# Gate projection of each head interleaved with the attention items

## The chip, the cores and the metric

The kernel runs on one core of a Trainium2 chip. The metric is the device time of one execution in microseconds (us); less is better. Engines: TensorE (PE) does matmuls into eight accumulator banks, VectorE (DVE), ScalarE (ACT) and GpSimd (POOL) work on elements, and the queues of SyncE (SP) and POOL issue the transfers.

## What is computed

One inference step with two layers, on 512 latent and 128 context tokens of width 2048. Layer 0 is attention with 16 query heads, 4 key and value heads and a gate; layer 1 is a gated recurrence, which the change does not touch. Cut from the reference:

```python
p = h @ w_in
q, k, v, g = split(p, [2048, 2560, 3072])      # widths 2048, 512, 512, 2048
q = rms_norm(q per head); k = rms_norm(k per head)
q = rope(q); k = rope(k)                       # latent tokens only
o = softmax(q k^T * HD**-0.5) v                # context: 128 keys; latent: 256 cached + 512 latent
out = (o * silu(g)) @ w_out
```

A latent token reads the 256 cached keys and its own 512; a context token reads the 128 context keys. Each sub-layer is led by a norm with shift and scale, which come from `silu(c) @ w_mod + b_mod`.

## The kernel before

Everything is float32. A product is made of three matmuls: every operand is split into a high part, rounded to TensorE's fast format, and a low part (operand less high part), and high x high, low x high and high x low are added in the accumulator (`mm3`, lines 184 to 186). `split_w` makes the two parts of a weight block: a cast on ACT (L179) and a subtraction on DVE (L180). The normed input of layer 0 stands as `hi` and `lo`, [128, 16, 644], in which every head of the attention result later takes the place of one sixteenth (latent tokens in columns 0 to 511, context tokens in 514 to 641).

The stretch that matters runs in stages. **Projections**: `gemm_nat` makes v, k and four blocks of 512 query columns in tokens x columns, in pairs of token tiles; `norm_rope` (from L454) copies each pair, squares it, reduces it per head (L463), scales it (L466), rotates it (L471 to L478) and stores it to DRAM (`q_s`, `k_s`; L485 on POOL's queue). The last pair is the single context tile. Its working tiles have two buffers. **Gate columns**: `gemm_T` makes eight blocks of 256 gate columns as columns x tokens, two accumulators of 322 tokens each per head; `g_evac` (L487) makes `g * (1 + tanh(g / 2))` and stores it per head to `g_s` in DRAM. **Attention**: 72 items, four query tiles of each of 16 heads and after each second head one item for the context tokens of both. Three functions treat an item: `stage_s` (L597) writes the scores into one of two 2-bank tiles `sp` and issues the softmax (maximum on DVE, L581; exponential on ACT, L584; normalisation on ACT or DVE by item); `stage_t` (L619) transposes the probabilities on TensorE and splits them; `stage_v` (L646), which works for two query tiles together, and so only at m = 1, 3 and 4 of a head's five kinds of item, multiplies with v and, at m = 3 and 4, with the gate (L664, L670), writing `hi` (L665, ACT) and `lo` (L666, POOL). The transposes of an item stand three items behind its scores (`AHEAD`). **Output projection** with `w_out` starts when the items are done and reads all of `hi` and `lo`.

Beside the projections and the gate columns runs `gemv` (L379), the vector product of the conditioning with `w_mod` for layer 1's shift and scale, as products on DVE: four blocks of 1024 columns, eight loads of 1 MB each, 16 partial sums per column and vector accumulated in place (L395). A block's 128 partition sums are then reduced on TensorE: the sums are split, eight matmuls of 512 columns with a selector (L403), a row copy on ACT (L406), eight transposes (L408). `background` spreads the loads over the projections and the gate columns.

Instructions of an engine run in the order in which they stand; a scheduler sets that order from the program and a priority. Loads of weights, of w_mod and of attention's inputs share four tiles `raw` of 1 MB.

## Time and profile before

| | us |
|---|---|
| median of 3 runs (lowest, highest) | 1954.33 (1953.74, 1959.88) |
| the profiled execution's own time | 1955.32 |
| its span | 1953.6 |
| PE busy | 1883.5 (96%) |
| DVE busy | 1323.9 (68%) |
| ACT busy | 865.0 (44%) |
| POOL busy | 133.1 (7%) |
| mean granted clock of TensorE, share of full | 0.991 |

In the trace the projections of layer 0 end at 428.69 us, the gate columns run to 664.6, the attention from there to 884.08, when the output projection begins. Times in the rows are microseconds from the start of the span; a row of a timeline has the start, the duration, the engine, the line, the operation, the tile written and the tiles read, the shapes and a count, and in brackets the idle time before it with what ended it. Matmuls overlap, so the time of one in a row of them is the distance between starts.

### The profile page before, as it was taken

How to read it: one execution, taken by the hardware profiler on the slowest of the kernel's cores; microseconds unless marked ns; L12 is line 12 of the kernel's file. 1: busy time of each engine (PE TensorE's matmuls, PEld its weight loads, DVE VectorE, ACT ScalarE, POOL GpSimd, SP SyncE). 2: the span in 40 equal slices, each digit the busy share in tenths (PEclk: the TensorE clock that was granted, in tenths of full speed). 3: DMA queues.
4: the chain of work that ended last, by engine and by line, in shares of the span. 5: the costliest groups of instructions: out<-in, count | busy, mean ns of one | idle time of the engine just before them, and what ended most of it. 6: DMA issues, size and time to landing. Idle time of an engine off the chain costs nothing.

```text
span 1953.6 us, 26764 instructions
## 1 busy us (share of the span) xinstructions
PE 1883.5 (96%) x10857; PEld 1673.2 (86%) x10857; DVE 1323.9 (68%) x1846; ACT 865.0 (44%) x1255; POOL 133.1 (7%) x212
## 2 busy tenths in 40 slices
PE   4999999999999899999999989899999999999996
PEld 1567887879999899998888889899999999987885
DVE  3237759758375389998857774875685675798645
ACT  4441223222121388881223565666456456742232
POOL 0000000000000001110000000110010010020000
PEclk9999999999999999999999999999999999999998
DMA  9996535536454212225636673323232232546445
GB/s 342 343 318 209 166 109 183 178 123 200 149 178 158 74 38 74 74 97 174 204 130 211 226 263 109 122 77 117 94 102 92 94 100 64 175 140 212 146 149 216
DMA packets 194892, 304.20 MB, mean 156 GB/s; under 512 B 7232, under 2 KB 124608, under 8 KB 191952
## 3 DMA queue, kind: packets, MB, share of 16 engines
q1 hardware_dynamic: 188800, 276.20, 42.6%
q0 software_dynamic: 5968, 26.28, 3.7%
q8 instruction: 85, 1.39, 0.3%
q14 instruction: 39, 0.32, 0.0%
HBM read 273.03 MB, written 29.43 MB: 155 GB/s over the span
## 4 chain that ended last, share of the span: by engine, by line
PE 83%; DVE 6%; ACT 5%; issue 2%; DMA 2%; SPq 1%; POOL 0%; DVEq 0%; ACTq 0%; POOLq 0%
PE pd L184 22%; PE pd L185 22%; PE pd L186 22%; PE pd L215 2%; PE pm L276 2%; PE pd L217 2%; PE pd L218 2%; PE ph L631 1%; PE pg L184 1%; ACT L937 1%; PE pg L186 1%; PE pg L185 1%; PE sp L184 1%; PE sp L186 1%; PE ph L184 1%
## 5 line engine op out<-in xcount | busy, mean ns | idle before, releaser
L179 ACT CAST wh<-raw 128x1024 fp32r<-128x1024 f32 x248 | 258.1, 1048 | 604.8 <-PE pd L186 323.6
L180 DVE TENSOR_TENSOR wl<-raw,wh 128x1024 fp32r<-128x1024 f32 x248 | 301.4, 1221 | 237.5 <-ACT wh L179 236.6
L184 PE MATMUL pd<-wh,hi 128*128 128x512 f32 x1040 | 410.4, 395 | 5.8 <-ACT pd L783 3.3
L185 PE MATMUL pd<-wl,hi 128*128 128x512 f32 x1040 | 409.9, 394 | 0.0
L186 PE MATMUL pd<-wh,lo 128*128 128x512 f32 x1040 | 409.7, 394 | 0.0
L184 PE MATMUL pd<-hi,wh 128*128 128x322 f32 x1280 | 399.2, 312 | 0.0
L186 PE MATMUL pd<-hi,wl 128*128 128x322 f32 x1280 | 397.0, 310 | 1.1 <-DVE wl L180 1.1
L185 PE MATMUL pd<-lo,wh 128*128 128x322 f32 x1280 | 397.5, 311 | 0.0
L186 PEld LDWEIGHTS pd<-hi,wl 128*128 128x128 f32 x1280 | 241.6, 189 | 1.6 <-DVE wl L180 1.6
L185 PEld LDWEIGHTS pd<-lo,wh 128*128 128x128 f32 x1280 | 242.2, 189 | 0.1
L184 PEld LDWEIGHTS pd<-hi,wh 128*128 128x128 f32 x1280 | 241.4, 189 | 0.5 <-ACT wh L179 0.3
L184 PEld LDWEIGHTS pd<-wh,hi 128*128 128x128 f32 x1040 | 195.5, 188 | 52.5 <-ACT pd L783 3.7
L186 PEld LDWEIGHTS pd<-wh,lo 128*128 128x128 f32 x1040 | 195.4, 188 | 45.9
L185 PEld LDWEIGHTS pd<-wl,hi 128*128 128x128 f32 x1040 | 195.4, 188 | 45.4 <-DVE wl L180 0.3
L741 DVE SCALAR_TENSOR_TENSOR ga<-raw,cT,ga 128x512 f32<-128x512 f32 x256 | 175.5, 744 | 15.2 <-DMA ga<-b_mod 12.4
L395 DVE SCALAR_TENSOR_TENSOR ga<-raw,cT,ga 128x1024 f32<-128x1024 f32 x120 | 149.7, 1278 | 28.1 <-DMA raw<-w_mod 27.5
L215 PE MATMUL pd<-hi,wh 128*128 128x256 f32 (+1 forms) x256 | 80.5, 314 | 6.4 <-ACT wh L179 4.7
L184 PE MATMUL pd<-xh,wh 128*128 128x322 f32 x256 | 81.1, 318 | 5.2 <-ACT xh L875 4.4
L185 PE MATMUL pd<-xl,wh 128*128 128x322 f32 x256 | 80.0, 313 | 0.0
L218 PE MATMUL pd<-hi,wl 128*128 128x256 f32 (+1 forms) x256 | 79.9, 312 | 0.0
L217 PE MATMUL pd<-lo,wh 128*128 128x256 f32 (+1 forms) x256 | 79.8, 312 | 0.0
L186 PE MATMUL pd<-xh,wl 128*128 128x322 f32 x256 | 79.8, 312 | 0.0
(233 smaller groups left out, 2807.3 us busy)
## 6 DMA issues: line engine op xcount, KB each, us to landing
raw<-w_mod SPq DMA_DIRECT2D x64, 1024.0 KB, 5.2
raw<-w_in_lru SPq DMA_DIRECT2D x40, 1024.0 KB, 5.3
raw<-w_in_attn SPq DMA_DIRECT2D x36, 1024.0 KB, 6.1
raw<-w_mod SPq DMA_DIRECT2D x64, 512.0 KB, 8.4
raw<-w_out_attn SPq DMA_DIRECT2D x20, 1024.0 KB, 6.0
raw<-w_out_lru SPq DMA_DIRECT2D x20, 1024.0 KB, 5.3
g_s<-qf POOLq DMA_DIRECT2D x16, 322.0 KB, 3.4
raw<-g_s SPq DMA_DIRECT2D x16, 322.0 KB
```

Of the source, the lines that this page charges most:

```text
L179: S.copy(wh, src)
L180: V.tensor_tensor(wl, src, wh.bitcast(F32), op=sub)
L184: PE.matmul(out, ah, bh, start=first, stop=False)
L185: PE.matmul(out, ah, bl, start=False, stop=False)
L186: PE.matmul(out, al, bh, start=False, stop=last)
L215: PE.matmul(outs[f], wh[:, c], hi[:, k, t], start=(k == 0 and first[f]), stop=False, skip_group_check=True)
L217: PE.matmul(outs[f], wh[:, c], lo[:, k, t], start=False, stop=False, skip_group_check=True)
L218: PE.matmul(outs[f], wl[:, c], hi[:, k, t], start=False, stop=(k == KT - 1), skip_group_check=True)
L276: PE.matmul(pm[32 * j:32 * j + 32], c32[:, kb * 4 + j], raw[:, j * 512:j * 512 + 512], start=(kb == 0), stop=(kb == 3))
L395: V.scalar_tensor_tensor(acc[c], w2[:, k2], cT[:, k, c:c + 1], acc[c], op0=mult, op1=add)
L631: PE.transpose(pt[:, c * 128:c * 128 + 128], P[:, b, c * 128:c * 128 + 128], ident)
L741: V.scalar_tensor_tensor(acc[:, c], raw[:, k4 * 512:k4 * 512 + 512], cT[:, kb * 4 + k4, c:c + 1], acc[:, c], op0=mult, op1=add)
```

## The change

The gate columns no longer have a stage of their own. A generator, `gate`, issues the 96 matmuls of one head after the other (16 weight blocks x 3, for each half of 322 tokens), with one accumulator bank per half; a head's weights are one load of 16 x 128 columns. The program calls `fill(n)`, which issues the next n gate matmuls, between the parts of the attention: 44 ahead of the first scores, and in each step 9 after the scores, 8 after the values and 8 after the transposes. The order of TensorE's instructions is that of the code; the other engines' order is still the scheduler's. The tile of scores has one buffer, probabilities two, their split transposes one, keys one. The gate of a head stays on chip (five buffers `gg`). Because gate matmuls still read `hi` and `lo`, the finished heads go to DRAM (`a_s`) until the gate has ended; then `load_a` fetches one head per step, with a cast on ACT into `hi` and a subtraction on POOL into `lo`. Heads whose values come after that are written straight away (`direct`). Transposes now stand one step, values two steps behind the scores.

`gemv` is called twice: shift beside the projections, in blocks of 1024, and scale beside the attention, in blocks of 512. Its reduction is now fp32 matmuls with two columns of the selector as the moving side.

```diff
@@ -31,10 +31,9 @@
 EPS = 1e-6
 QSCALE = HD ** -0.5
 NORM = "dadad"
-AHEAD = 3
-QV = (1, 2, 3)
-QO = (2, 2, 3)
-PB = 4
+GGB = 5
+LEAD = 44
+FILL = (9, 8, 8)
 GATE2 = (1, 2, 5)
...
-    g_s = [tc.dram_tile([128, TW], F32, name=f"g_s{h}") for h in range(NH)]
+    a_s = [tc.dram_tile([128, TW], F32, name=f"a_s{h}") for h in range(NH)]
...
+    def gemv(part, p, ps_, width):
+
+        nk, nf = 2048 // width, width // 128
+        for col in range(0, D, width):
+            acc = [p.tile([128, width], F32, name=f"ga{c}", tag=f"ga{c}") for c in range(2)]
+            for kb in range(KT // nk):
+                w = rawp.tile([128, 2048], F32, name="raw", tag="raw")
+                wk = w.rearrange("p (k n) -> p k n", k=nk)
+                SY.dma_start(wk, i["w_mod"][1, kb * nk * 128:(kb + 1) * nk * 128,
+                                            part * D + col:part * D + col + width]
+                             .rearrange("(k p) n -> p k n", p=128))
+                for k2 in range(nk):
+                    k = kb * nk + k2
+                    for c in range(2):
+                        if k == 0:
+                            V.tensor_scalar(acc[c], wk[:, k2], cT[:, k, c:c + 1], None, op0=mult)
+                        else:
+                            V.scalar_tensor_tensor(acc[c], wk[:, k2], cT[:, k, c:c + 1], acc[c],
+                                                   op0=mult, op1=add)
+                    if k2 % 2 or nk == 2:
+                        yield
...
+            pg = ps_()
+            for k in range(nf):
                 for c in range(2):
...
+                    PE.matmul(pg[:, 2 * k:2 * k + 2], acc[c][:, k * 128:k * 128 + 128],
+                              sel[:, c].bitcast(F32), start=(c == 0), stop=(c == 1))
...
+    gv = gemv(0, pb, lambda: psd()[:, 0], 1024)
...
-        credit[0] += 32 / 36
+        credit[0] += 32 / 19
...
-    def g_evac(acc, gb):
-        for f in range(2):
-            th = pb.tile([128, 2, 512], F32, name="qs", tag="qs", bufs=2)
-            gg = pb.tile([128, 2, 512], F32, name="qf", tag="qf", bufs=2)
-            S.activation(th[:, :, :TH], acc[f][:, :, :TH], AF.Tanh, scale=0.5)
-            V.scalar_tensor_tensor(gg[:, :, :TH], th[:, :, :TH], 1.0, acc[f][:, :, :TH], op0=add, op1=mult)
-            G.dma_start(g_s[gb * 2 + f].rearrange("p (h t) -> p h t", h=2), gg[:, :, :TH])
...
-    for gb in range(8):
-        g_evac(gemm_T(w_in, 3072 + gb * 256, background), gb)
...
-    psS = pool("psS", 2, PSUM, stack=xs)
+    psS = pool("psS", 1, PSUM, stack=xs)
...
+    psG = pool("psG2", 2, PSUM, stack=xs)
...
+    ggs, over, direct = {}, [], {}
+
+    def gate():
+
+        raws, ws = {}, {}
+
+        def load(h):
+            raws[h] = rawp.tile([128, 2048], F32, name="raw", tag="raw")
+            SY.dma_start(raws[h].rearrange("p (k n) -> p k n", k=KT),
+                         w_in[:, 3072 + h * 128:3200 + h * 128].rearrange("(k p) n -> p k n", p=128))
+
+        def split(h, half):
+            ws[h, half] = split_w(raws[h][:, half * 1024:half * 1024 + 1024])
+
+        load(0)
+        split(0, 0)
+        for h in range(NH):
+            if h + 1 < NH:
+                load(h + 1)
+            gg = pc_.tile([128, TW], F32, name="gg", tag="gg", bufs=GGB)
+            for e in range(2):
+                t = slice(e * TH, e * TH + TH)
+                acc = psG.tile([128, 512], F32, name="pg", tag="pg")
+                for q, half in enumerate((e, 1 - e)):
+                    if (e, q) == (0, 0):
+                        split(h, 1)
+                    elif (e, q) == (1, 0) and h + 1 < NH:
+                        split(h + 1, 0)
+                    wh, wl = ws[h, half]
+                    for k8 in range(8):
+                        k = half * 8 + k8
+                        c = slice(k8 * 128, k8 * 128 + 128)
+                        for n, (x, y) in enumerate(((wh, hi), (wh, lo), (wl, hi))):
+                            PE.matmul(acc[:, :TH], x[:, c], y[:, k, t], start=(q == 0 and k8 == 0 and n == 0),
+                                      stop=(q == 1 and k8 == 7 and n == 2))
+                            yield
+                S.activation(gg[:, t], acc[:, :TH], AF.Tanh, scale=0.5)
+                V.scalar_tensor_tensor(gg[:, t], gg[:, t], 1.0, acc[:, :TH], op0=add, op1=mult)
+            ggs[h] = gg
+        over.append(1)
+
+    gf = gate()
+
+    def fill(n):
+        for _ in range(n):
+            next(gf, None)
...
+    def load_kv(j):
         c = slice(j * 128, j * 128 + 128)
         raw = rawp.tile([128, 2048], F32, name="raw", tag="raw")
-        kx = raw[:, :896].rearrange("p (t d) -> p t d", d=128)
-        vx = pc_.tile([128, 7, 128], F32, name="vx", tag="vx")
-        for x, cache, scr in ((kx, "cache_k", k_s), (vx, "cache_v", v_s)):
-            SY.dma_start(x[:, 0:2], i[cache][0, 0, :, j, :].rearrange("(t p) d -> p t d", p=128))
-            SY.dma_start(x[:, 2:7], scr[:, c].rearrange("(t p) d -> p t d", p=128))
-        kh = pc_.tile([128, 896], F32R, name="kh", tag="kh", bufs=2)
-        kl = pc_.tile([128, 896], F32R, name="kl", tag="kl", bufs=2)
+        x2 = raw[:, :1792].rearrange("p (a t d) -> p a t d", a=2, d=128)
+        for a, (cache, scr) in enumerate((("cache_k", k_s), ("cache_v", v_s))):
+            SY.dma_start(x2[:, a, 0:2], i[cache][0, 0, :, j, :].rearrange("(t p) d -> p t d", p=128))
+            SY.dma_start(x2[:, a, 2:7], scr[:, c].rearrange("(t p) d -> p t d", p=128))
+        kraw[j] = x2
...
+    def load_q(h):
+        qx = pc_.tile([128, 5, 128], F32, name="qx", tag="qx")
+        SY.dma_start(qx, q_s[:, h * 128:h * 128 + 128].rearrange("(t p) d -> p t d", p=128))
+        qraw[h] = qx
...
+        while h not in ggs:
+            fill(1)
+        if m == 1:
+            direct[h] = bool(over)
+        vh, vl = vs[h // 4]
+        po = psh()
+
+        def put_y(h, t, p):
+            y = ggs[h][:, t]
+            V.scalar_tensor_tensor(y, p, 0.5, y, op0=mult, op1=mult)
+            if direct[h]:
+                S.copy(hi[:, h, t], y)
+                G.tensor_tensor(lo[:, h, t], y, hi[:, h, t].bitcast(F32), op=sub)
...
+            for e in range(2):
+                put_y(h - 1 + e, slice(PO, TE), po[:, e * 128:e * 128 + 128])
+                if not direct[h - 1 + e]:
+                    G.dma_start(a_s[h - 1 + e][:, :TE], ggs[h - 1 + e][:, :TE])
+
+    back = iter(range(NH))
+
+    def load_a():
+
+        h = next(back, None)
+        if h is None or direct.get(h):
             return
-        yv = qs_[h][3]
-        if m == 3:
-            V.scalar_tensor_tensor(yv, po, 0.5, qs_[h][2][:, :512], op0=mult, op1=mult)
-            S.copy(hi[:, h, :512], yv)
-            G.tensor_tensor(lo[:, h, :512], yv, hi[:, h, :512].bitcast(F32), op=sub)
-        else:
-            h0 = h - 1
-            for e in range(2):
-                V.scalar_tensor_tensor(yv[:, e * 128:e * 128 + 128], po[:, e * 128:e * 128 + 128], 0.5,
-                                       qs_[h0 + e][2][:, PO:TE], op0=mult, op1=mult)
-            y2 = yv[:, :256].rearrange("p (h t) -> p h t", h=2)
-            S.copy(hi[:, h0:h0 + 2, PO:TE], y2)
-            V.tensor_tensor(lo[:, h0:h0 + 2, PO:TE], y2, hi[:, h0:h0 + 2, PO:TE].bitcast(F32), op=sub)
+        raw = rawp.tile([128, 2048], F32, name="raw", tag="raw")
+        r = raw[:, :TE]
+        SY.dma_start(r, a_s[h][:, :TE])
+        S.copy(hi[:, h, :TE], r)
+        G.tensor_tensor(lo[:, h, :TE], r, hi[:, h, :TE].bitcast(F32), op=sub)
...
+    gv = gemv(1, pc_, psh, 512)
+    with tc.manual_schedule(engines={mybir.EngineType.PE}):
+        load_kv(0)
+        load_q(0)
+        fill(LEAD - 12)
+        attn_k(0)
+        attn_q(0)
+        fill(12)
+        for n in range(len(items) + 2):
+            it = items[n] if n < len(items) else None
+            if it:
+                h, m = it
+                if m == 0 and h + 1 < NH:
+                    load_q(h + 1)
+                    if h % 4 == 3:
+                        load_kv(h // 4 + 1)
+                stage_s(it)
+                if it == last[h] and h + 1 < NH:
+                    if h % 4 == 3:
+                        attn_k(h // 4 + 1)
+                    attn_q(h + 1)
+            fill(FILL[0])
+            if n >= 2:
+                h, m = items[n - 2]
+                if m == 0 and h % 4 == 0:
+                    attn_v(h // 4)
+                stage_v((h, m), *done.pop(n - 2))
+            fill(FILL[1])
+            if 0 <= n - 1 < len(items):
+                done[n - 1] = stage_t(items[n - 1])
+            fill(FILL[2])
+            if n % 2:
+                next(gv, None)
+            if over:
+                load_a()
+        for _ in gv:
+            pass
+        for _ in range(NH):
+            load_a()
```

DVE at the start of the attention, the last query block's norm (its last step is L475) up to the low parts of the first head's keys (`kl`) and queries (`ql`); `ga` are sums of the vector product. In the changed kernel the first maximum (L614) stands three vector products behind these rows:

```order
L461 TENSOR_TENSOR qf<-qf,rr 128x512
L475 TENSOR_TENSOR qs<-qf,gain_q 128x512
L393 TENSOR_SCALAR ga_3303<-raw,cT 128x512
L393 TENSOR_SCALAR ga_3304<-raw,cT 128x512
L579 TENSOR_TENSOR kl<-ph,kh 128x512
L579 TENSOR_TENSOR kl<-ph,kh 128x384
L395 SCALAR_TENSOR_TENSOR ga_3303<-raw,cT,ga_3303 128x512
L395 SCALAR_TENSOR_TENSOR ga_3304<-raw,cT,ga_3304 128x512
L395 SCALAR_TENSOR_TENSOR ga_3303<-raw,cT,ga_3303 128x512
L607 TENSOR_TENSOR ql<-ph,qh 128x512
L607 TENSOR_TENSOR ql<-ph,qh 128x128
```

Before, the first maximum (L581) follows at the end of the gate columns; `wl<-ph` is the low part of the queries:

```order
L492 SCALAR_TENSOR_TENSOR qf<-qs,pd 128x2x322 x2
L417 TENSOR_TENSOR gt<-pd,VA 128x16
L419 SCALAR_TENSOR_TENSOR scale_153<-gt,VA 128x2x8
L545 TENSOR_TENSOR kl<-ph,kh 128x512
L545 TENSOR_TENSOR kl<-ph,kh 128x384
L575 TENSOR_TENSOR wl<-ph,wh 128x512
L575 TENSOR_TENSOR wl<-ph,wh 128x128
L575 TENSOR_TENSOR wl<-ph,wh 128x512
L581 TENSOR_REDUCE mx<-sp 128x1 x2
```

The last step of the last query block's norm stood 80 rows ahead of `kl` and stands now three rows ahead of it.

ACT near the end of the attention in the changed kernel (L617 exponential, L622 normalisation, L662 cast of the transposed probabilities, L547 tanh of the gate, L711 cast of a head that was loaded back):

```order
L711 CAST hi<-raw 128x642 x4
L617 ACTIVATE P,sm<-sp,mx 128x768
L711 CAST hi<-raw 128x642
L622 ACTIVATE P<-P,rs 128x768
L711 CAST hi<-raw 128x642 x2
L662 CAST pth<-ph 128x3x128 x2
L547 ACTIVATE gg<-pg 128x322
L711 CAST hi<-raw 128x642
L662 CAST pth<-ph 128x3x128 x2
L711 CAST hi<-raw 128x642
L617 ACTIVATE P,sm<-sp,mx 128x768
L711 CAST hi<-raw 128x642 x3
```

Before, in the last items (L584 exponential, L589 normalisation, L634 cast of the transposed probabilities, L179 cast of w_out):

```order
L584 ACTIVATE P,sm<-sp,mx 128x768
L634 CAST pth<-ph 128x3x128 x2
L584 ACTIVATE P,sm<-sp,mx 128x768
L179 CAST wh<-raw 128x1024
L589 ACTIVATE P<-P,rs 128x768
L584 ACTIVATE P,sm<-sp,mx 128x768
L634 CAST pth<-ph 128x3x128 x2
L179 CAST wh<-raw 128x1024
L584 ACTIVATE P,sm<-sp,mx 128x768
L634 CAST pth<-ph 128x3x128 x2
L589 ACTIVATE P<-P,rs 128x768
L634 CAST pth<-ph 128x3x128
```

Twelve casts of 642 columns now stand among the exponentials; before, casts of w_out stood there.

## Rows read from the trace of the kernel before

**Rows 1.** The page's part 1: engine, busy us, share of the span, instructions.
```profile
PE 1883.5 (96%) x10857; PEld 1673.2 (86%) x10857; DVE 1323.9 (68%) x1846; ACT 865.0 (44%) x1255; POOL 133.1 (7%) x212
```

**Rows 2.** Busy by stretch: length, PE, PEld, DVE, ACT, POOL, PEclk, DMA, GB/s.
```profile
429.00:665.00 236.00, 234.91 (x1574) 231.04 (x1573) 136.92 (x150) 53.05 (x61) 12.29 (x18) 1.00 0.48 161
...
670.00:683.00 13.00, 9.21 (x43) 8.74 (x43) 8.16 (x14) 7.03 (x14) 2.09 (x1) 0.74 0.39 118
...
699.00:867.00 168.00, 166.68 (x1256) 160.57 (x1256) 152.39 (x334) 143.47 (x323) 23.07 (x16) 1.00 0.22 67
867.00:888.00 21.00, 18.59 (x125) 16.14 (x124) 14.74 (x32) 12.96 (x28) 3.47 (x3) 1.00 0.34 120
```

**Rows 3.** PE timeline, 428.5 to 431.6 us: start us, duration us, instruction.
```profile
428.69 0.62 PE L403 MATMUL pd<-wh,sel 128*2 128x512 f32 x2
...
430.54 0.32 PE L184 MATMUL pd<-hi,wh 128*128 128x322 f32 x1
```

**Rows 4.** PE timeline, 698.5 to 884.6 us: scores of two items, output projection.
```profile
698.95 0.34 PE L184 MATMUL sp<-kh,wh 128*128 128x384 f32 x1
...
867.09 0.34 PE L184 MATMUL sp<-kh,wh 128*128 128x384 f32 x1
...
884.08 0.39 PE L184 MATMUL pd<-wh,hi 128*128 128x512 f32 x1
```

**Rows 5.** PE timeline, 437 to 439 us: twelve gate matmuls lie between.
```profile
437.13 0.31 PE L184 MATMUL pd<-hi,wh 128*128 128x322 f32 x1
...
438.91 0.31 PE L184 MATMUL pd<-hi,wh 128*128 128x322 f32 x1
```

**Rows 6.** PE timeline, 664 to 678 us: end of the gate, first scores.
```profile
666.81 0.65 PE L408 MATMUL pd<-ident,row 2*128 2x2 f32 x8 [1.09 <-ACT row L406]
...
676.31 0.69 PE L184 MATMUL sp<-kh,wh 128*128 128x384 f32 x1 [3.79 <-ACT P L584]
...
677.44 0.52 PE L184 MATMUL sp<-kh,wh 128*128 128x384 f32 x1
677.76 0.52 PE L185 MATMUL sp<-kl,wh 128*128 128x384 f32 x1
```

**Rows 7.** ACT timeline, 664 to 684 us.
```profile
674.43 0.94 ACT L552 CAST vh<-vx 128x896 fp32r<-128x896 f32 x1 [2.68 <-DMA vx<-v_s]
675.27 0.90 ACT L584 ACTIVATE P<-sp,mx 128x768 f32<-128x768 f32 x1
```

**Rows 8.** PE timeline, 50.5 to 53 us: fp32 matmuls with two columns.
```profile
50.84 0.95 PE L288 MATMUL pm<-sel,row 128*128 128x2 f32 x8
```

**Rows 9.** ACT timeline, 424 to 426 us: the last query block's first copy.
```profile
424.70 1.01 ACT L459 COPY qf<-pd 128x1024 f32<-128x1024 f32 x1 [1.71 <-PE pd L186]
```

**Rows 10.** DVE timeline, 426 to 460 us: norm and rotation of that block.
```profile
427.60 1.21 DVE L463 TENSOR_REDUCE ss<-qs 128x8 f32<-128x1024 f32 x1
...
442.12 1.22 DVE L466 TENSOR_TENSOR qf<-qf,rr 128x1024 f32<-128x1024 f32 x1
...
444.52 0.69 DVE L471 TENSOR_TENSOR qs<-qf,ropeC_q 128x512 f32<-128x512 f32 x1
445.12 0.76 DVE L476 TENSOR_TENSOR t<-qf,ropeS_q 128x256 f32<-128x256 f32 x2
```

**Rows 11.** DMA issues: out<-in, queue, count, KB each, median us to landing.
```profile
raw<-w_mod SPq DMA_DIRECT2D x64, 1024.0 KB, 5.2
...
raw<-y_s SPq DMA_DIRECT2D x16, 321.0 KB, 3.8
raw<-q_s SPq DMA_DIRECT2D x16, 320.0 KB, 3.3
...
q_s<-qs POOLq DMA_DIRECT2D x4, 256.0 KB, 2.9
```

**Rows 12.** DVE timeline, 664 to 684 us: one maximum.
```profile
678.64 0.96 DVE L581 TENSOR_REDUCE mx<-sp 128x1 f32<-128x768 f32 x1 [0.61 <-PE sp L186]
```

**Rows 13.** Groups by line, 699 to 867 us: busy us, mean ns, idle before.
```profile
L666 POOL TENSOR_TENSOR lo<-raw,hi 128x512 fp32r<-128x512 f32 x13 | 16.7, 1287 | 140.2 <-ACT hi L665 140.2
```

More of the change, by code (lines that the diff above doesn't have):

```diff
@@ L680, in hybrid_step @@
             items.append((h, 4))
+    last = {h: (h, 4 if h % 2 else 3) for h in range(NH)}
     done = {}
[L682 to L700 removed]
```

159 lines of the change are left out of this document (40 added, 119 removed).

## Prediction

> **What bounds the kernel now.** The page's first part comes first: TensorE is busy for 96% of the span [rows 1]. The busy time by stages then shows where the rest is [rows 2]: in the gate stretch (429 to 665) TensorE has hardly a gap, and in the steady attention (699 to 867) 166.7 of 168 us, while DVE has 152.4. Between them, from 670 to 683, TensorE works 9.2 of 13 us at a mean granted clock of 0.74, which is half level (1.2 GHz) for 2 x 0.26 x 13 = 6.8 us and costs 3.4 us.
>
> So the stretch that the change rewrites, from the first matmul of a vector reduction at 428.69 to the first of the output projection at 884.08 [rows 3, 4], is 455.4 us. I take it apart:
> - Gate columns: twelve matmuls of 322 columns take 438.91 - 437.13 = 1.78 us [rows 5], 0.1485 us each; 1536 of them are 228.1 us.
> - Attention: 59 items lie between two score matmuls at 698.95 and 867.09 [rows 4]: 2.85 us per item, 205.2 us for 72.
> - Vector reductions: 1.85 us for the eight wide matmuls [rows 3] and 0.58 us for the eight transposes (666.81 to 667.39, by their length of 0.65 [rows 6]); 2.43 us, three times, 7.3 us.
> - The rest, 14.8 us, is loss: mostly the passage from gate to attention, where the scores at 676.31 waited 3.79 us for an exponential [rows 6] that stood on ACT behind a cast of v waiting 2.68 us for its load [rows 7].
>
> That 14.8 us is all that the change can win on TensorE, whose matmuls stay the same. An interleaved gate can fill softmax waits; but the waits must not merely move.
>
> **The change, part by part.**
>
> *Gate columns and attention items.* The same 1536 and the same items: 228.1 + 205.2. Nothing shows why a matmul of 322 columns should cost more between scores; half-empty banks cost no columns.
>
> *The vector product's reduction.* Line 402 of the changed kernel sends unsplit sums through fp32 matmuls with two moving columns: 16 per 1024-wide block, 8 per 512-wide one. The nearest row is the same shape elsewhere, four calls, recorded as eight, in 0.95 us [rows 8], 0.24 each. The lower bound is a transpose with two columns, 0.65 / 8 = 0.08 [rows 6]. I take 0.24, the upper end, since operand and type agree. Of the 64, 48 lie in the stretch: 11.4 us (at the lower bound 3.9) for 7.3. The other 16 cost 3.8 in the projections in place of 2.4: +1.4. The row copies and casts that go were on ACT and DVE, beside other work.
>
> *The start.* Before, the last query block's norm and rotation ran for some 30 us under gate matmuls which had nothing to do with it. Now only 44 gate matmuls stand before the first scores, and these need all of it. Count from 424.5, where that block's first pair ends (its copy starts at 424.70 [rows 9]). ACT copies and squares, 2.0. DVE then, for each of two pairs, reduces (1.21), scales (1.22), multiplies twice 0.69 and twice 0.76, adds (1.22) [rows 10], with 0.7 of small operations: 14.5 for both; the single context tile takes half-size steps, 2.8. Then the store of q, 2.9, and the load of the first head, which reads all tokens, 3.3 [rows 11]; transposes, cast, one vector product ahead on DVE, and the low part: about 2.5; the scores themselves 1.05. Together 29.1. In it TensorE has: the projection until 428.69, 4.2; 44 x 0.1485 = 6.5; twelve transposes 1.3; reduction 3.8, already counted; scores 1.05. Without the reduction that is 13.1, with it 16.9. So **12 us of stall** (bounds 6, if the two DVE pairs overlap better with the projection, and 16). A stall of that size lasts longer than the 3.79 [rows 6] after which the clock stood at half level (0.32 us a matmul of 384 columns, 677.44 to 677.76 [rows 6]), so I add the same 3.4 us (bounds 0 and 7).
>
> *The interleaved steps.* A step has 25 gate matmuls, 3.7 us, and an item, 2.85: 6.56 us. DVE's share of an item is 152.4 / 59 = 2.58 us [rows 2]; with a split half, two gate products and the vector product's, some 4.8. One score buffer now: scores to maximum (0.96 [rows 12]) to exponential (0.90 [rows 7]), about 2.2 us with the handing over, and 16 to 34 other matmuls lie between. So TensorE stays fed unless DVE stands still: a w_mod load takes 5.2 us [rows 11] and DVE's product queues in order ahead of the next maximum; at about 2.1 us of other DVE work in front, it holds the maximum 3.1 us, against 2 to 4 us of cover. I put **3 us** on all of it (bounds 0 and 25: half of 16 loads x 3.1).
>
> *The tail.* The gate ends near step 60; the last dozen items have one score buffer and no gate matmuls. Where no value stage is issued (8 of 18 items), scores wait for maximum and exponential, 2.2 us, with six transposes (0.66) for cover: 1.6 us idle, six times, 9.6. Beside that the load-backs share ACT with the exponentials. Each of 13 goes load (3.8 for the same size [rows 11]), ACT cast, then POOL's subtraction, 1.29 us for 512 columns [rows 13], so 1.6 for 642; four buffers turn, POOL being the slowest. Four loads are there when the gate ends and free their buffers at 2.3, 3.9, 5.5 and 7.1 us; the fifth lands at 6.1 and frees at 8.7, so the ninth lands near 12.9. In ACT's order casts five to nine stand before the second exponential: it comes at 13.6 instead of 9.3, 4.3 us late. The last items' drain into the output projection, with w_out's load and casts behind the load-backs, adds 4. **18 us** (bounds 4, if the casts run ahead of need, and 24).
>
> The clock in that tail: from 867 to 888 TensorE idled 2.4 of 21 us in short pieces at a granted clock of 1.00 [rows 2], so I sum the tail at full level. The Trainium skill ("TensorE: Matmul & The Clock Gate", section "A second HAM failure mode: psum-queue depth-cycling") says the opposite of such gaps: a TensorE that idles briefly between groups of matmuls drops its clock again and again. By that rule the sum would be higher by the price of the clock rival below.
>
> *Taken away at nothing:* 16 stores and loads of g; they lay under the gate matmuls and attention, and the stores and loads of y replace 13 of them.
>
> **Sum.** 228.1 + 205.2 + 11.4 + 12 + 3.4 + 3 + 18 = 481.1, against 455.4: +25.7, and +1.4 before it: +27. On the profiled execution's own 1955.3 us that is 1982; the median of the runs, 1954.33, is 1.0 lower, so **1981 us**.
>
> **Rivals.** About 0.3% (6 us) is what a measurement of this kernel can tell from no change.
> - *Everything covered (faster).* Place: the first scores and the tail. If norm and load of the last block finish under the projection's own matmuls, and load-backs run ahead of the exponentials, only the 3 us stay: 228.1 + 205.2 + 11.4 + 3 = 447.7, +1.4: -6.3, 1948 us. For it speaks that ACT and DVE have slack in the interleaved part; against it that TensorE's fill is fixed at 44 matmuls, 6.5 us. It decides if all stalls together stay below 455.4 - 444.7 - 1.4 = 9.3 us. Chance 0.07; between that and 6 us slower, with half the start and little tail, 0.10 for no difference.
> - *Start paid, tail hidden.* 12 + 3.4 + 3 and 4 of drain: 467.1, +13.1, 1967 us. It holds if casts and exponentials interleave better than I have them, or if work ahead of the scores is fetched early. Chance 0.20.
> - *DVE becomes the bound.* If w_mod waits show at half of 16 x 3.1 us, 25 instead of 3: 2003 us. For it: order on DVE; against: 4.8 of 6.56 us busy. Chance 0.10.
> - *Clock.* If half of the tail's 62 us (44.3 work and 18 stall) runs at half level, 31 x 0.5 = 15.5 more: 1996 us. Against it the row from 867 to 888. Chance 0.08.
> - The forecast itself, 1981, has 0.45 (own range 1970 to 1992).
>
> **Numbers.** Faster 0.07, same 0.10, slower 0.83. The range 1958 to 2003 leaves out the covered case, half of the no-difference case and the far end of the DVE case, 0.17 or so.
>
> **What would show it.** In the changed kernel's profile: idle before the transposes of k, released by ACT's square of the context tile, and before the first scores, released by ql on DVE, together some 12 us around 430 to 455, followed by a half-level clock; 6.5 us steps with TensorE full; line 402's groups at 0.24 us; after the last line-544 matmul, idle before scores released by the exponential, about 1.6 us each on steps without values, and one long one behind the fifth to ninth casts. I am wrong if the distance from the end of the projections to the output projection is near 450, if the start's idle is a few microseconds, or if gaps recur through the interleaved steps behind line 395 on DVE.

## The result and the profile after

| | before | after |
|---|---|---|
| median of 4 runs, us | 1956.72 (1953.74 to 1959.88) | 1986.01 (1980.34 to 1989.77) |
| span of the profiled execution | 1953.6 | 1983.2 |
| first scores, after the end of the projections | | 23.0 |
| end of projections to output projection | 455.4 | 476.7 |

The changed kernel takes 1.0153 times as long (95% interval 1.0126 to 1.0180). TensorE is busy 95% of the span where it was 96% [rows 1], 10 us longer in all:

```profile
PE 1893.8 (95%) x10921; PEld 1693.3 (85%) x10921; DVE 1328.0 (67%) x1930; ACT 860.0 (43%) x1257; POOL 135.2 (7%) x215
```

The PE timeline of the changed kernel at the end of the projections and at the output projection, which answer to [rows 3, 4] (L402 is the reduction; 32 records are sixteen calls):

```profile
433.98 0.40 PE L185 MATMUL pd<-wh,lo 128*128 128x512 f32 x1
434.21 3.63 PE L402 MATMUL pd<-sel,ga 128*128 128x2 f32 x32
...
457.23 0.45 PE L183 MATMUL sp<-kh,qh 128*128 128x384 f32 x1 [2.16 <-ACT qh L606]
```

```profile
910.92 0.39 PE L183 MATMUL pd<-wh,hi 128*128 128x512 f32 x1
```

The projections end at 434.21 instead of 428.69 and the output projection begins at 910.92 instead of 884.08. The profiled execution is thus 5.5 us later in the projections, 21.3 us in the stretch and 2.8 us behind it, together the 29.6 us of the two spans. Busy time by stretch (length, PE, PEld, DVE, ACT, POOL, PEclk, DMA share, GB/s), as in [rows 2]:

```profile
434.20:457.20 23.00, 15.63 (x89) 14.97 (x87) 19.14 (x44) 5.70 (x11) 2.44 (x4) 0.78 0.22 77
457.20:470.00 12.80, 9.50 (x46) 9.18 (x47) 9.15 (x13) 3.48 (x6) 2.05 (x1) 0.73 0.63 191
470.00:853.00 383.00, 383.00 (x2752) 382.23 (x2752) 280.15 (x520) 183.27 (x366) 18.13 (x19) 1.00 0.36 106
853.00:862.00 9.00, 3.22 (x23) 2.94 (x22) 3.75 (x8) 7.17 (x14) 8.49 (x6) 0.80 0.78 207
862.00:910.80 48.80, 40.78 (x270) 36.97 (x268) 32.86 (x70) 31.67 (x71) 11.69 (x13) 0.93 0.37 134
```

From 470 to 853, where gate matmuls and items alternate, TensorE has no idle time at all. All its idle time in the stretch lies at the two ends, 434 to 470 and 853 to 911. The waits of TensorE in these (us in total, times, longest us), first the start, then the tail:

```profile
PE ph L576 <- ACT qs L455: 5.2, 1, 5.2
PE sp L185 <- DVE ql L607: 3.3, 1, 3.3
PE sp L183 <- ACT qh L606: 2.2, 1, 2.2
```

```profile
PE sp L183 <- ACT P L617: 11.6, 5, 5.8
PE ph L184 <- DVE ptl L663: 0.7, 2, 0.4
PE ph L659 <- ACT P L622: 0.5, 1, 0.5
```

At the start TensorE idles 10.7 us and runs part of the rest at half level (the rows' mean granted clock is 0.78 up to 457.2 and 0.73 up to 470). In the tail 11.6 us go to scores that wait for an exponential, since the one tile of scores has to be read first; the longest of these waits, 5.8 us, is the first.

### The profile page after: what moved, and what is told of

It is laid out like the page before. It is cut to its first block, busy times and chain, and to the rows that moved or that the text cites. A ratio compares the mean times of both kernels' runs of the same rounds, so it can differ in the third digit from the quotient of the medians.

```text
span 1983.2 us, 26998 instructions
## 1 busy us (share of the span) xinstructions
PE 1893.8 (95%) x10921; PEld 1693.3 (85%) x10921; DVE 1328.0 (67%) x1930; ACT 860.0 (43%) x1257; POOL 135.2 (7%) x215
## 4 chain that ended last, share of the span: by engine, by line
PE 75%; issue 11%; ACT 5%; DVE 5%; DMA 2%; SPq 1%; POOL 1%; DVEq 0%; ACTq 0%; POOLq 0%
PE pd L183 18%; PE pd L184 18%; PE pd L185 18%; PE pg L544 5%; PE pd L214 2%; PE pd L216 2%; PE pd L217 2%; PE pm L275 2%; PE pg L183 1%; ACT L976 1%; PE pg L185 1%; PE pg L184 1%; PE ph L659 1%; DVE wl L179 1%; PE ph L184 1%
## 5 line engine op out<-in xcount | busy, mean ns | idle before, releaser
L179 DVE TENSOR_TENSOR wl<-raw,wh 128x1024 fp32r<-128x1024 f32 x248 | 301.9, 1221 | 218.4 <-ACT wh L178 217.2
L183 PE MATMUL pd<-hi,wh 128*128 128x322 f32 x768 | 239.6, 312 | 0.0
L184 PE MATMUL pd<-lo,wh 128*128 128x322 f32 x768 | 238.4, 310 | 0.0
L185 PE MATMUL pd<-hi,wl 128*128 128x322 f32 x768 | 238.0, 310 | 0.0
L395 DVE SCALAR_TENSOR_TENSOR ga<-raw,cT,ga 128x512 f32<-128x512 f32 (+1 forms) x180 | 162.5, 931 | 12.8 <-DMA raw<-w_mod 12.6
L544 PE MATMUL pg<-hi,wl 128*128 128x322 f32 x512 | 163.3, 319 | 0.0
L544 PE MATMUL pg<-lo,wh 128*128 128x322 f32 x512 | 162.9, 318 | 0.0
L544 PE MATMUL pg<-hi,wh 128*128 128x322 f32 x512 | 162.5, 317 | 0.0
L184 PEld LDWEIGHTS pd<-lo,wh 128*128 128x128 f32 x768 | 145.3, 189 | 0.0
L617 ACT ACTIVATE P<-sp,mx 128x768 f32<-128x768 f32 (+1 forms) x80 | 63.6, 797 | 98.3 <-DVE mx L614 98.3
L544 PEld LDWEIGHTS pg<-hi,wl 128*128 128x128 f32 x512 | 98.5, 192 | 0.0
L544 PEld LDWEIGHTS pg<-hi,wh 128*128 128x128 f32 x512 | 98.4, 192 | 0.0
```

The lines of the kernel that those rows point to most:

```text
L179: V.tensor_tensor(wl, src, wh.bitcast(F32), op=sub)
L183: PE.matmul(out, ah, bh, start=first, stop=False)
L184: PE.matmul(out, ah, bl, start=False, stop=False)
L185: PE.matmul(out, al, bh, start=False, stop=last)
L395: V.scalar_tensor_tensor(acc[c], wk[:, k2], cT[:, k, c:c + 1], acc[c], op0=mult, op1=add)
L544: PE.matmul(acc[:, :TH], x[:, c], y[:, k, t], start=(q == 0 and k8 == 0 and n == 0), stop=(q == 1 and k8 == 7 and n == 2))
```

## The experiments

All times are us; the stretch is that from the end of the projections to the output projection, the tail that from the last gate matmul to it. In the two runs with the late vector product, its second reduction (3.6) lies ahead of the stretch.

Each row's times are from one profiled execution, the ratio is from all of a run's executions. How far such times scatter can be read off where the program is the same: in the eight kernels with the change's projections these end between 429.2 and 436.5, and in the three with the change's gate, items and tail (the change, e5_wide and e12_norot) the tail is 55.7 to 58.3. A few us there are therefore no effect yet. The first scores scatter less: 22.8 to 23.5 in the seven kernels that leave the order of the start as it is. The profiled execution of e4_both was the shortest of its four (2071.26, the others 2079.6 to 2080.0), that of e11_all the longest (1997.1, the others 1986.4 to 1987.8). In the change the scores of 12 items stand behind the last gate matmul; with 140 gate matmuls first and 24 in a step it is 13, with 20 in a step it is one.

| run | to first scores | to last gate matmul | tail | stretch | ratio to before |
|---|---|---|---|---|---|
| the change | 23.0 | 418.8 | 57.9 | 476.7 | 1.0153 |
| e1_lead | 36.6 | 414.3 | 65.4 | 479.7 | 1.0147 (1.0117 to 1.0176) |
| e2_two | 23.5 | 519.4 | 60.8 | 580.2 | 1.0656 (1.0633 to 1.0678) |
| e3_noback | 23.0 | 420.2 | 55.1 | 475.3 | 1.0127 (1.0100 to 1.0155) |
| e4_both | 23.0 | 515.8 | 48.9 | 564.7 | 1.0624 (1.0594 to 1.0653) |
| e5_wide | 22.8 | 418.5 | 55.7 | 474.1 | 1.0098 (1.0080 to 1.0115) |
| e6_late | 20.4 | 413.7 | 68.3 | 482.0 | 1.0207 (1.0187 to 1.0228) |
| e7_late_lead | 31.6 | 405.3 | 72.6 | 477.9 | 1.0169 (1.0148 to 1.0191) |
| e8_slow | 23.0 | 453.5 | 25.9 | 479.4 | 1.0170 (1.0148 to 1.0192) |
| e9_early | 36.7 | 411.4 | 66.2 | 477.6 | 1.0154 (1.0130 to 1.0178) |
| e10_tail | 23.1 | 418.6 | 63.6 | 482.2 | 1.0179 (1.0158 to 1.0200) |
| e11_all | 36.6 | 411.9 | 74.7 | 486.6 | 1.0185 (1.0158 to 1.0211) |
| e12_norot | 18.4 | 415.8 | 58.3 | 474.1 | 1.0124 (1.0100 to 1.0148) |

**The start: more gate matmuls first, then memory of its own.**

```diff
-LEAD = 44
-FILL = (9, 8, 8)
+LEAD = 140
+FILL = (8, 8, 8)
```

> 140 gate matmuls instead of 44 stand ahead of the first scores, and 24 instead of 25 in a step, so that the gate ends within two steps of where it ended. Theory: the start's loss (15.8 us between 434.2 and 462.6 in the changed kernel's trace, idle and half-level clock) is due to scores that need the last query block's norm with too little other work for TensorE; 96 more gate matmuls (14.3 us) cover it, so the loss falls by 12 to 14 us and the time from the end of the projections to the output projection falls from 476.7 to about 463 to 466 us. Rival: the idle is set by the memory and banks which the projections' stage still holds, so that gate matmuls beyond the first 44 wait as well; then the loss stays at 12 us or more and the time within 3 us.

The scores came 13.6 us later, and the 96 added matmuls are worth 14.3: hardly any wait was covered, it moved. The PE timeline shows where:

```profile
461.71 0.64 PE L544 MATMUL pg<-hi,wh 128*128 128x322 f32 x1 [7.42 <-DVE gg L548]
```

The third accumulator is the first one used again, and it waits until a product on DVE has emptied it. The next run gave the gate's tiles memory that the norm had not used:

```diff
+    es = ExitStack()
+    pg_ = pool("pg_", 1, stack=es)
...
-            gg = pc_.tile([128, TW], F32, name="gg", tag="gg", bufs=GGB)
+            gg = pg_.tile([128, TW], F32, name="gg", tag="gg", bufs=GGB)
```

> As the run with 140 gate matmuls ahead of the first scores and 24 in a step, with one edit more: the tiles for the gate of a head lie in memory of their own instead of memory that the projections' norm still uses. Theory: the 7.4 us wait inside those 140 matmuls came from the tanh of the first accumulator, which had to wait (1.70 us on ACT, behind the norm's last step on DVE) for that memory, and from the product behind it; with its own memory the accumulators are emptied while the norm runs, so that wait falls below 2 us and the time from the end of the projections to the first scores from 36.6 to 28 to 31 us. Rival: DVE, busy with the norm for some 17 us in its fixed order, is the limit, whatever the memory; then the wait stays above 5 us.

The wait stayed (first scores after 36.7 instead of 36.6): the rival holds. The load of the tanh's table, which in e1_lead waited 1.70 us for the norm's last step (L475), did not wait now, and the tanh ran 1.8 us nearer to the projections' end, but DVE reached the product no sooner (26.2 us after it, 26.4 before), behind the norm and four products of the vector product (L397 in this kernel, L550 the gate's product):

```profile
455.16 5.05 DVE L397 SCALAR_TENSOR_TENSOR ga<-raw,cT,ga 128x512 f32<-128x512 f32 x4
460.13 0.48 DVE L550 SCALAR_TENSOR_TENSOR gg<-gg,pg 128x322 f32<-128x322 f32 x1
```

**The start: shorten the chain on DVE.**

```diff
-        credit[0] += 32 / 19
+        credit[0] += 36 / 19
...
-            if n % 2:
+            if n % 2 and n >= 5:
```

> The vector product's second block is finished some three weight loads before the projections end (36 / 19 instead of 32 / 19 per load), and its part beside the attention begins at step 5 instead of step 1. Theory: the start's 15.8 us are one chain on DVE: it stood 3.1 us for the reduction at 434.6, then ran the last query block's norm, then three products (3.9 us) ahead of ql. With both out of the way the first scores come 6 to 7 us earlier after the end of the projections, and the stretch from there to the output projection falls from 476.7 to 466 to 471 us (the sixteen matmuls of 3.6 us that it no longer holds included). Rival: the chain runs over the store of q and the memory that the projections hand over; then the first scores come less than 3 us earlier, reduction apart.

A miss by the first scores: they came 2.6 us nearer to the projections' end (20.4) where the theory wanted 6 to 7, although the reduction of 3.6 now lies ahead of that end. To the end of the first item's scores, which holds the wait for `ql`, the way did shrink more, from 28.4 to 23.4 (by 1.4 without the reduction). What stands in the way here is the rival's store: ACT's square of the context tile waited 3.17 us for one, and on DVE `ql` 1.36 us (DVE timeline of this run):

```profile
460.35 1.16 DVE L579 TENSOR_TENSOR kl<-ph,kh 128x512 fp32r<-128x512 f32 x2 [0.73 <-ACT kh L578]
462.86 0.89 DVE L607 TENSOR_TENSOR ql<-ph,qh 128x512 fp32r<-128x512 f32 x2 [1.36 <-DMA q_s<-qs]
```

The vector product that was put off ended in the tail, which took 68.3. Together with the longer lead:

> The last edit together with 140 gate matmuls ahead of the first scores and 24 in a step. Alone, the 140 matmuls only moved the wait into the gate: its third accumulator waited 7.4 us for a product on DVE behind the norm. Theory: that product now stands behind the norm alone, so the wait shrinks to 1 to 4 us and the scores wait for nothing: start loss 3 to 7 us, and the time from the end of the projections to the output projection is 457 to 465 us. Rival: the wait in the gate stays above 6 us, since ACT and DVE reach it only after the norm; then no gain over the run with the late vector product alone.

The wait in the gate was still 6.5 us from start to start, as the rival says; the last gate matmul came 13.5 earlier than in the change (9.9 without the reduction), but the tail is 14.7 longer, some 2.7 of it for the one item more. Neither run settles the start, so the last one took work out of the norm itself, the rotation of the last block's latent queries:

```diff
-            if ms[0] < 4:
+            if ms[0] < 4 and rot:
...
-        norm_rope(gemm_nat(w_in, n * 512, background), "q", q_s[:, n * 512:n * 512 + 512])
+        norm_rope(gemm_nat(w_in, n * 512, background), "q", q_s[:, n * 512:n * 512 + 512], rot=n < 3)
```

> The changed kernel with the rotation of the last query block's latent pairs left out (scaled by the gain alone, so these four heads' queries are not rotated): on DVE 2 x (1.38 + 1.52 + 1.22 - 1.22) = 5.8 us less in the chain between the end of the projections and the first scores, and nothing else moved. Theory: the start's loss is that chain on DVE, at whose end the casts of the keys and the low parts of the queries wait for the norm's memory; then the first scores stand 4.5 to 6 us nearer to the end of the projections (17 to 18.5 us after it instead of 23.0). Rival: the wait is for the store of q to DRAM or for the accumulator of the context tile, which the norm's arithmetic does not set; then they come less than 2 us earlier.

5.8 us less on DVE brought the first scores 4.6 us nearer (18.4), inside the theory's range, and the end of the first item's scores 3.3 us (25.1). A store of q begins only behind its pair's arithmetic, so this run alone moves the store too and does not exclude the rival. The rows do for the changed kernel: from 437.9 to `ql` DVE has one idle piece, 0.27 us, and none for a store. In e12_norot the store begins to show on DVE, by way of ACT's square:

```profile
446.96 0.69 DVE L458 TENSOR_REDUCE ss<-qs 128x4 f32<-128x512 f32 x1 [0.96 <-ACT qs L455]
```

So the norm's arithmetic on DVE sets most of the start; the changed kernel's DVE timeline shows the chain, from the reduction's result to `ql`:

```profile
437.88 0.18 DVE L409 TENSOR_TENSOR shift<-pd,VA 128x16 f32<-128x16 f32 x1 [3.10 <-PE pd L402]
...
438.25 1.21 DVE L458 TENSOR_REDUCE ss<-qs 128x8 f32<-128x1024 f32 x1
...
444.43 1.23 DVE L473 TENSOR_TENSOR qs<-qs,t 128x1024 f32<-128x1024 f32 x1
...
450.78 1.21 DVE L473 TENSOR_TENSOR qs<-qs,t 128x1024 f32<-128x1024 f32 x1
...
454.08 0.69 DVE L475 TENSOR_TENSOR qs<-qf,gain_q 128x512 f32<-128x512 f32 x1
454.69 0.88 DVE L393 TENSOR_SCALAR ga<-raw,cT 128x512 f32<-128x512 f32 x2
455.50 1.16 DVE L579 TENSOR_TENSOR kl<-ph,kh 128x512 fp32r<-128x512 f32 x2
456.57 3.89 DVE L395 SCALAR_TENSOR_TENSOR ga<-raw,cT,ga 128x512 f32<-128x512 f32 x3
460.39 0.88 DVE L607 TENSOR_TENSOR ql<-ph,qh 128x512 fp32r<-128x512 f32 x2
```

and ACT, which waits for it and for the store of the first pair:

```profile
449.23 0.60 ACT L455 ACTIVATE qs<-pd 128x512 f32<-128x512 f32 x1 [4.15 <-DMA q_s<-qs]
...
454.88 0.97 ACT L578 CAST kh<-ph 128x512 fp32r<-128x512 f32 x2 [2.56 <-DVE qs L475]
```

The norm's last step ends at 454.8; only then are the keys cast (2.56 us of waiting for L475, although they need nothing from it). That their tile takes memory which the norm gives up is inferred; no run gave the keys other memory, but the gate's tile waited for the same step and no longer did with memory of its own (e9_early). Then three products stand between `kl` and `ql`.

**The tail: a second tile of scores, load-backs left out, both.**

```diff
-    psG = pool("psG2", 2, PSUM, stack=xs)
+    psG = pool("psG2", 1, PSUM, stack=xs)
+    gacc = psG.tile([128, 2, 512], F32, name="pg", tag="pg")
...
-                acc = psG.tile([128, 512], F32, name="pg", tag="pg")
+                acc = gacc[:, e]
...
-        sp = psS.tile([128, 2, 512], F32, name="sp", tag="sp")
+        turn[0] ^= 1
+        sp = gacc if over and turn[0] else psS.tile([128, 2, 512], F32, name="sp", tag="sp")
```

> When the gate has ended, its two accumulator banks serve as a second tile of scores, used in turn with the first; nothing else is changed. Theory: of some 20 us lost between the last gate matmul (852.99) and the output projection (910.92), about 10 us are scores that wait for the exponential of the one tile (gaps of 0.9, 1.4, 2.7 and 2.0 us after 862), and these go: the tail falls from 57.9 to 48 to 50 us. Rival: the load-backs on ACT and POOL set the tail; then the first gap of 6 us stays, the others only move to the transposes, and the tail stays at 55 us or more.

The tail did not shrink (60.8), as the rival says: the scores' later waits went, and the transposes and values waited instead, some 9 us in all. The first gap (4.5 us) stayed, but it stands before the second tile, which the gate's last product has to read first. And the edit changed something else: two halves in one tile are no longer two accumulators. The gate now waits before a half until the product has read the other one, 30 times, at most 4.2 us, 65.6 us together; the mean granted clock from 452 to 949 is 0.93, and the run is 98 us longer. This is what one tile per half buys in the change. PE timeline of this run (L549 is the product):

```profile
505.87 0.42 PE L545 MATMUL pg<-hi,wh 128*128 128x322 f32 x1 [2.65 <-DVE gg L549]
...
521.41 0.42 PE L545 MATMUL pg<-hi,wh 128*128 128x322 f32 x1 [1.10 <-DVE gg L549]
...
536.97 0.41 PE L545 MATMUL pg<-hi,wh 128*128 128x322 f32 x1 [2.91 <-DVE gg L549]
```

```diff
-        if h is None or direct.get(h):
+        if h is None or h < NH:
```

> The 13 heads that were stored are not loaded back (load, cast and subtraction left out, so the output projection multiplies what was in hi and lo before); all else as in the changed kernel. Theory: the 6.05 us gap right after the gate's end is the exponential behind casts that wait for loads, and goes; the scores' own waits stay: the tail falls from 57.9 to 50 to 53 us. Rival: the one tile of scores alone sets the tail, and it stays within 2 us of 57.9.

The tail was 2.8 us shorter, 55.1, between theory and rival; the first wait shrank from 5.8 to 3.1 us and the others stayed:

```profile
PE sp L183 <- ACT P L617: 8.9, 5, 3.1
```

e5_wide, with all its load-backs, has a tail of 55.7 and a first wait of 4.9, so 2.8 us is the most that the load-backs cost here, and it is not clear of the scatter.

> Both edits: no load-backs, and two tiles of scores after the gate. Theory (two causes that add up): the tail falls to 41 to 45 us, near the 14 items' own work of 38 to 40 us. Rival: a third cause, such as one buffer of split transposes or keys, holds it; then it stays above 48 us.

48.9: against the run with the second tile alone 11.9 us less, but in the shortest of four executions; the medians of the two runs lie only 4.3 us apart. In these profiles the second tile is worth nothing while load-backs stand on ACT, the load-backs cost at most 3 us while there is one tile, and only both give something; a rest of 9 us over the items' own work stays, as the rival expected. Which buffer holds it was not tried.

**The tail: deeper, or shorter.** Closing the accumulators' pool at the gate's end avoids the shared tile; transposes and values stand one step further behind from there on.

```diff
+        if over and not more:
+            gs.close()
+            more.append(pool("psS2", 1, PSUM, stack=xs))
+        turn[0] ^= 1
...
+            wait = bool(over) and not skipped
+            skipped = skipped or wait
-            if n >= 2:
+            if n >= 2 and vi < len(items) and not wait:
```

> The changed kernel up to the gate's end; then the accumulator banks' pool is closed and a second tile of scores opened in its place, and transposes and values move one step further behind the scores. Theory: the tail's loss of 20 us comes from three waits that cover for each other: the one tile of scores, the transposes only one step behind, and casts of load-backs ahead of exponentials; the first two go, the first gap of 6 us stays: the tail falls from 57.9 to 47 to 51 us. Rival: the load-backs on ACT alone set it; then the tail stays at 55 us or more.

63.6: the theory fell. The waits for the exponential went (one of 0.2 us is left behind a first gap of 4.3 us, which is for the gate's product here), but values now waited for the split transposes, 10.8 us in all. The other way is to keep gate matmuls until the last items:

```diff
-FILL = (9, 8, 8)
+FILL = (7, 7, 6)
```

> 20 gate matmuls in a step instead of 25, so that the gate ends some ten steps later, near the last items; nearly all heads are then stored and loaded back, and most load-backs stand beside the output projection. Theory: what is lost in the tail is lost on items without gate matmuls between their stages (scores behind the one tile, transposes one step behind, casts ahead of exponentials), so with about 4 such items instead of 12 the tail's loss falls from 20 us to 8 to 12, the output projection's wait for the first heads included, and the time from 434 to the output projection's last wait falls by 6 to 12 us. Rival: load-backs are what costs, and more of them behind the gate's end cost more: 3 us or more slower than the changed kernel.

The theory fell: the tail's items lose less now, but the stretch is 2.7 us longer. That is the rival's direction, though 2.7 us, and 3.0 between the medians, are not clear of the scatter. The output projection stood 10.85 us. PE, ACT and SP's queue in this run (the wait is for w_out's weights, whose load was issued at 907.94, behind eleven load-backs):

```profile
914.21 1.22 PE L183 MATMUL pd<-wh,hi 128*128 128x512 f32 x2 [10.85 <-ACT wh L178]
```

```profile
910.49 0.73 ACT L711 CAST hi<-raw 128x642 fp32r<-128x642 f32 x1 [5.58 <-DMA raw<-a_s]
913.11 1.99 ACT L178 CAST wh<-raw 128x1024 fp32r<-128x1024 f32 x2 [1.90 <-DMA raw<-w_out_attn]
```

```profile
886.88 20.96 SPq L710 DMA_DIRECT2D raw<-a_s  x11
907.94 0.39 SPq L169 DMA_DIRECT2D raw<-w_out_attn  x1
```

**The reductions beside the projections.** L402's form was undone for the two wide blocks:

```diff
+            if part == 0:
+                pd_ = psd()
+                for c in range(2):
+                    ah, al = split_w(acc[c])
...
+                        for b in range(2):
+                            PE.matmul(pd_[:2, b], sel[:, c], x[:, b * 512:b * 512 + 512], start=(c + j == 0),
```

> The two blocks of the vector product beside the projections are reduced as in the kernel before (split, eight wide matmuls, row copy, eight transposes); the rest is the changed kernel. In the changed kernel and the four runs so far, a stretch of matmuls at half level followed the sixteen two-column matmuls near 303 us in four of five profiles, and those near 434 us in all five. Theory: TensorE's clock falls because of those blocks; then in this run no half-level stretch follows the reductions, and the gate's first matmuls run at 0.148 us: the time from 300 to the first scores falls by 2 to 5 us. Rival: the clock falls because of the waits around them (gate's start, projections); then the half-level stretches stay.

The half-level stretch near 308 went, the one near 438 stayed, there behind a wait of 2.6 us for the row copy. For the first block this fits the theory, and e11_all, with the same reductions, has no half level there either; it is no proof, since two of eleven profiles with the two-column form have none. The second block does not tell. Stretches of 4 us around the first reduction, the change, then this run (columns as above; the ninth number is PEclk):

```profile
300.00:304.00 4.00, 4.00 (x20) 3.25 (x18) 0.00 (x0) 0.00 (x0) 0.00 (x0) 1.00 0.78 259
304.00:308.00 4.00, 4.00 (x36) 3.91 (x35) 0.64 (x1) 1.04 (x1) 0.00 (x0) 1.00 0.02 7
308.00:312.00 4.00, 4.00 (x13) 3.10 (x12) 4.00 (x6) 0.00 (x0) 0.00 (x0) 0.60 0.00 0
```

```profile
300.00:304.00 4.00, 4.00 (x19) 3.14 (x18) 3.89 (x4) 0.00 (x0) 0.00 (x0) 1.00 0.27 58
304.00:308.00 4.00, 4.00 (x18) 2.33 (x17) 3.07 (x4) 3.76 (x4) 0.00 (x0) 1.00 1.01 385
308.00:312.00 4.00, 4.00 (x24) 3.10 (x23) 3.63 (x5) 0.09 (x1) 0.00 (x0) 1.00 0.97 333
```

The median is 1975.05 and the ratio's interval does not meet that of the change, so this run is about 0.5% shorter. How much of it the edit gave is open: of the two profiles' difference 2.2 us lie in the projections, 2.2 in the tail and 5.4 behind the output projection's start, and in the last two the program is the same. e2_two, with the two-column form, ended its projections 2.8 us earlier still.

**All cures at once**: e5's reductions, e9's start, e10's tail, and the load-backs' cast on POOL.

```diff
-        S.copy(hi[:, h, :TE], r)
+        G.tensor_copy(hi[:, h, :TE], r)
```

> All together: wide reductions beside the projections, 140 gate matmuls first with memory of their own for the gate, the tail with two tiles of scores one step further behind, and the load-backs' cast on POOL instead of ACT. Theory: the three losses are separate and their cures add up: 5 to 10 us from the reductions, 6 to 8 from the start, 9 to 14 from the tail, which leaves 1955 to 1966 us, at best even with the kernel before. Rival: a cure in one place moves the wait to another (load-backs on POOL then come too late for the output projection, as they did with 20 gate matmuls a step); then 1970 us or more.

1987.66 us: the rival holds, the cures did not add up; in the profiled execution the tail took 74.7, with one item more than e10_tail's 63.6. No version here beats the kernel before.

## Why the prediction was right

Forecast 1981 in 1958 to 2003, measured 1986.01; +27 was the sum, +29.6 the spans. The mechanism held: little to gain between the seams, a stall at the start, a loss in the tail. That the sum came out so near is in part luck, in three of its terms:

- *Stretch*: 481.1 forecast, 476.7 measured.
- *Interleaved steps*: forecast 2.85 per item, 0.1485 per gate matmul and 3 us of stalls. From 470 to 853 there was no stall: 1457 gate matmuls took 222 us by their starts (0.152), 58 items 156 (2.69 each) and reductions 5. That is 7 us less than the forecast for these 383 us, and 4 us less than the same matmuls and items at the prices before; this is the change's gain. Only some of it can be waits that the gate's matmuls now fill, since the kernel before idles 1.3 us in its 59 items [rows 2]; the rest is open. DVE did not become the bound: the vector product waited 3.5 us in all for its loads, not 25:

```profile
L395 DVE SCALAR_TENSOR_TENSOR ga<-raw,cT,ga 128x512 f32<-128x512 f32 x114 | 81.7, 742 | 3.5 <-DMA raw<-w_mod 3.4
```

- *Start*: 28.4 us from the end of the projections to the end of the first item's scores, with 12.5 of work, so 15.9 lost; forecast 12 + 3.4. The size was right by luck, one step of it was wrong: the forecast's chain holds 2.9 + 3.3 us for the last store of q and the load of the first head behind it, but that head's queries come from the first query block, and their load was issued 3.9 us before the projections' end. Without these 6.2 us the same count would have given 6 us of stall in place of 12. What filled their place: DVE took 22.6 us from the first reduction (432.20) to the norm's end in place of 17.3, 3.1 of them waiting for L402's result, and from there to the scores that need `ql` 6.4 us passed in place of 2.5, with five products ahead of `ql` where one was counted. TensorE's wait at the transposes of k (5.2 us, for ACT's square, which waited 4.15 for a store) was foreseen in its place, but lies beside this chain.
- *Tail*: some 14 items' work at 2.69 and one reduction are an estimated 39.5 of 57.9 us, so 18.4 lost; forecast 18. Two of the three causes were as written, scores waiting for the one tile (four waits, 5.9 us; forecast six, 9.6) and one long wait behind casts of load-backs (5.8; forecast 4.3). The third, 4 us of drain into the output projection, did not come: its first matmul waited for nothing, and the last items had three waits of at most 0.5 us. Two stretches at half level, summed at full level in the forecast, cost some 3.5 us instead. ACT timeline, then the exponential that the 5.8 us wait is for:

```profile
854.18 0.73 ACT L711 CAST hi<-raw 128x642 fp32r<-128x642 f32 x1 [0.28 <-DMA raw<-a_s]
856.42 0.73 ACT L711 CAST hi<-raw 128x642 fp32r<-128x642 f32 x1 [1.51 <-DMA raw<-a_s]
...
858.27 0.73 ACT L711 CAST hi<-raw 128x642 fp32r<-128x642 f32 x1
...
859.77 0.73 ACT L711 CAST hi<-raw 128x642 fp32r<-128x642 f32 x1
860.41 0.90 ACT L617 ACTIVATE P<-sp,mx 128x768 f32<-128x768 f32 x1
```

  The forecast summed the two as separate terms, and they are not: in the runs, taking either away gave nothing or at most 3 us.
- *Reduction*: 3.63 us for sixteen calls, 0.23 each, forecast 0.24. What was missed is the clock behind it: most of the projections' +5.5 (forecast +1.4) is this block, its half-level stretch, and a wait of TensorE near 150 us (3.8, before 1.5) for a store of v, with a half-level stretch behind it too. Other profiles of the same code have 1.0 to 4.1 there; e2_two, with 1.4 and no half level in either place, ended its projections only 0.6 us later than the kernel before.
- *Clock rival*: in the tail TensorE worked at half level in two stretches of some 3.5 us each. The clock fell once inside the wait of 5.8 us and once behind one of 1.7, and not at the one of 2.4 between them. That is a loss of some 3.5 us, where the rival has 15.5. The Trainium skill ("TensorE: Matmul & The Clock Gate", "A second HAM failure mode: psum-queue depth-cycling") says that brief idling between groups of matmuls makes the clock go back and forth between its two levels. The tail agrees in kind, with two falls in 58 us.

## What to carry to other kernels

Interleaving two stages can win only what both lose inside, and where TensorE is busy in both, that is little: here the two steady stretches idled 1.1 and 1.3 us [rows 2], and the gain was some 4. Its price stands at the seams: what the second stage's first item needs of the first stage's last block, and what the last items do when the filler has run out. Before merging, follow the chain on the in-order engine beside TensorE (here the norm on DVE) from the end of the stage ahead to the first item, and count how much filler can run without that engine: accumulators that it must empty are the limit, not matmuls. Waits that cover each other, such as one tile of scores and casts on the same queue, do not add up: with one of them gone, the next took most of its place.

## What the runs showed of the hardware that was not expected

- Sixteen back-to-back fp32 matmuls with two moving columns, in an otherwise gapless stretch of projections, had a half-level stretch behind them or from their middle on (in the changed kernel a granted clock of 0.60 over 4 us, rows of 304 and 308 above), in 9 of the 11 profiles with that form (all but e2_two and e7_late_lead) near the first such block; eight wide matmuls in its place had none, in the three profiles that have them (the kernel before, e5_wide and e11_all).
- A product on DVE can take far longer beside a subtraction on POOL: three products of 512 columns, 0.74 us each as a rule, took 3.89 us while POOL's ran (one of them 2.57), and two took 3.73 in e12_norot. No run tries it by itself, but the profiles agree: of such products 4943 have no POOL instruction beside them and took at most 0.76 us; 51 took over 0.8 us, and each of these ended 0.54 to 0.56 us after a subtraction or cast on POOL, as if it had been held until then. In the change 1.8 us of the wait for `ql` come from this. Subtractions on DVE that read an accumulator (`ptl`, `ql`) were not longer beside POOL. The change's POOL row, then e12_norot's DVE rows:

```profile
456.77 2.48 POOL L587 TENSOR_TENSOR vl<-raw,vh 128x896 fp32r<-128x896 f32 x1 [0.88 <-ACT vh L586]
```

```profile
451.27 3.73 DVE L395 SCALAR_TENSOR_TENSOR ga<-raw,cT,ga 128x512 f32<-128x512 f32 x2
454.92 1.14 DVE L578 TENSOR_TENSOR kl<-ph,kh 128x512 fp32r<-128x512 f32 x2
```
